# Values of three retention heads by a two-level product scheme, and a third of the convolution's taps on other engines

## The chip, the cores and the metric

The kernel runs on one core of a Trainium2 chip. Such a core has a matrix engine (TensorE, PE in the profile, its weight loads as PEld), three engines for element-wise work (VectorE as DVE, ScalarE as ACT, GpSimd as POOL), and queues that start DMA transfers (those of SyncE, SP, and those that GpSimd issues). Matrix products go to PSUM, where the kernel keeps eight tiles of 128 partitions x 512 float32; all other data are in SBUF. The metric is the device time of one execution, as the median of several runs.

## The reference

Two layers of a mixer block on x of 512 tokens x 1024 channels, in float32. In each layer h = RMSNorm(x), one input projection of h feeds three branches, and an output projection adds to x:

```
v = a * sigmoid(b);  y = depthwise conv of v, 31 taps, + bias;  layer norm, silu, * silu(gate)
retention, 4 heads:  q, k of 256 channels (rotary), v of 512 channels;
    o = sum over all tokens of (q.k) * decay(distance) * v;  normalised, * silu(gate)
attention, 16 heads of 64 in 4 groups, window of 128 tokens on both sides, with sinks
x = x + W_out( g0 * W_conv y_conv + g1 * W_ret y_ret + g2 * W_attn y_attn )
```

What the change touches are the values v of the retention heads, v[token, channel] = sum over the 1024 input channels of h[token, i] * W[i, channel], 512 channels a head; and the convolution, for each channel a sum of 31 products of a tap's weight with the shifted v.

## The kernel before

**Data.** Activations lie with channels on the partitions: eight tiles of 128 channels x 512 tokens for x, h and so on. To keep float32 accuracy with matmul operands of type float32r, every operand is split in a high part (`hh`, `wh`: a cast by ScalarE) and a low part (`hl`, `wl`: the rest), and `mm3()` makes three matmuls of each product: high x high, high x low, low x high.

**Weights.** `raw()` loads a weight tile of 128 x 1024 from HBM through SyncE's queue into pool `wraw` (four buffers). `split()` makes `wh` and `wl` of 512 columns each (eight buffers per pool): ScalarE casts, then VectorE subtracts. For kinds listed in `BY_DMA` the subtraction goes another way: ScalarE writes the negated high part into `wl`, and a DMA issued by GpSimd adds the raw weights to it.

**Products.** `columns()` gives 128 channels x 512 tokens: weights are the loaded (stationary) operand, 512 tokens move. `tokens()` gives 128 tokens x 512 channels for each of four token blocks: the activations are loaded, the weights move, 8 k-tiles x 4 blocks x 3 matmuls of 512 columns. `two()` makes two `columns()` results at once by a Strassen scheme in Winograd's form: seven products instead of eight, on halves of the tokens (256 moving columns) and halves of the input channels, with sums of weights made by VectorE in pool `ws` and sums of activations (`th_`, `tl_`) made once per layer in `sums()`. Three PSUM tiles a, b, e are used again within a call: b for the second, fifth and seventh product, after VectorE has read the one before.

**Retention.** `head()` runs four times a layer. Head 0 takes its values by `tokens()` from the unnormalised input and scales them later. Heads 1 to 3 (the second to fourth) call `queries()` (two `two()` calls and rotary), then `tokens()` and `split_values()`, then `toeplitz()` for the decay table (two tiles of pool `wide`), score products, value products, a normalisation (GpSimd makes the reciprocal root) and a gate. Between these steps stand filler pieces of other work, placed by `HEAD_FILL`: convolution input C, convolution taps T, gates R, S, L, K and so on.

**Convolution.** `taps()` runs for each of eight channel groups a layer: it fetches v into `pad` (one buffer, with zero borders set by GpSimd), and VectorE makes 31 multiply-adds one after the other into `yt`. `conv_stats()` later reads all eight results in the attention stage, and `conv_finish()` in the layer's last stage.

**The order.** The program records all operations first. The class `Plan` then runs a model of five engines with its own prices (`cost()`) and puts each engine's operations in a fixed order: always the ready one with the lowest priority number, which is the TensorE time planned so far plus an offset (`SPLIT_EARLY`, `EVAC_EARLY`, `LOAD_EARLY` make it earlier, `TAPS_LATE` of 150,000 ns makes the taps fill whatever is free). A tile gets a buffer of its pool in the order of the program. On the chip every engine works through its fixed list in order and waits where an operand is not there; all instructions carry the line of `issue()` (L342), so rows are told apart by tile names.

Of the kernel before, what the change touches and what calls it, by code (L numbers as in the profile page):

```python
# [13 lines left out]
AF = mybir.ActivationFunctionType  # L14
ALU = mybir.AluOpType
# [7 lines left out]
TAPS = 31  # L23
PADW = S + TAPS - 1
HALF_TAPS = TAPS // 2


POOLS = {"big": 12, "pp": 8, "mid": 2, "th": 2, "wide": 2, "pad": 1, "yt": 2, "wraw": 4, "wh": 8, "wl": 8, "ws": 2, "half": 3}
PSUM_POOLS = {"pc": 4, "ps": 4}
# [26 lines left out]

BY_DMA = ("xs", "or", "a22")

# [101 lines left out]
class Plan:  # L160
# [23 lines left out]
    def cost(self, engine, method, kw):  # L184
# [14 lines left out]
        if engine == "gpsimd":  # L199
            if kw.get("op") == ALU.pow:  # L200
                return 290 + 166 * n
            return 75 + 2.25 * n
        if method in ("bn_stats", "tensor_reduce"):
# [175 lines left out]
class Builder:  # L379
# [37 lines left out]

    def th(self):
        return self.tile("th", [P, S])

    def half(self):
# [14 lines left out]

    def raw(self, key):
        nc, i = self.nc, len(self.keys)
        self.keys.append(key)
        raw = self.tile("wraw", [P, 1024])  # L440
        with nc.urgency(2 * FIRST + FIRST_STEP * (i - 0.1) if i < 4 else LOAD_EARLY):
            nc.sync.dma_start(out=raw, in_=self.io["wpk"][i])
        return raw
# [22 lines left out]
    def two(self, col0, col1, out0, out1, func0=None, func1=None):  # L466
# [53 lines left out]
        if func1 is not None:  # L520
            nc.scalar.activation(out=out1, in_=out1, **func1)


# [130 lines left out]
    def take(self, k):  # L654

        nc = self.nc
        u = self.t2()
        nc.vector.tensor_scalar(out=u, in0=self.x[k], scalar1=self.ng[:, k:k + 1], scalar2=None, op0=ALU.mult)
        self.hilo(self.uh[k], self.ul[k], u)
        with nc.urgency(SQUARES_LATE):  # L660
            if k == 0:
                nc.scalar.activation(out=self.acc, in_=self.x[k], func=AF.Square)
            else:
                sq = self.th()
                nc.scalar.activation(out=sq, in_=self.x[k], func=AF.Square)
                nc.vector.tensor_tensor(out=self.acc, in0=self.acc, in1=sq, op=ALU.add)
# [91 lines left out]
    def conv_in(self, c):  # L758

        nc = self.nc  # L760
        th = self.th()
        v = self.pp()
# [4 lines left out]
    def taps(self, c):  # L767

        nc, prm = self.nc, self.prm
        pad = self.tile("pad", [P, PADW])  # L770
        y = self.tile("yt", [P, S])
        nc.gpsimd.memset(ap=pad[:, 0:HALF_TAPS], constant=0.0)
        nc.gpsimd.memset(ap=pad[:, HALF_TAPS + S:PADW], constant=0.0)
        self.fetch("vd", c, pad[:, HALF_TAPS:HALF_TAPS + S])
        with nc.urgency(TAPS_LATE):
            for k in range(TAPS):
                w = prm[:, O_DW + c * TAPS + k:O_DW + c * TAPS + k + 1]
                if k == 0:
                    nc.vector.tensor_scalar(out=y, in0=pad[:, k:k + S], scalar1=w, scalar2=prm[:, O_CB + c:O_CB + c + 1], op0=ALU.mult, op1=ALU.add)
                else:  # L780
                    nc.vector.scalar_tensor_tensor(out=y, in0=pad[:, k:k + S], scalar=w, in1=y, op0=ALU.mult, op1=ALU.add)
            self.keep("y", c, y)
# [21 lines left out]
    def head(self, h, first):  # L804
# [10 lines left out]
        else:  # L815
            qk = self.queries(h, self.cos, self.sin)
            v = self.split_values(self.tokens(R_V + h * 512))
        (qkh, qkl), (vh, vl) = qk, v
# [125 lines left out]
    def conv_finish(self):  # L944
# [3 lines left out]
        for k in range(8):  # L948
            th = self.th()
            y = self.fetch("yc", k, self.tile("yt", [P, S]))  # L950
# [86 lines left out]
    def attention(self):  # L1037
# [6 lines left out]
        def AG(c):  # L1044
            th = self.th()
            p = self.proj(A_GATE + c * P)
# [211 lines left out]
```

## Time and profile before

| | |
|---|---|
| median of 3 runs | 1946.38 us (1946.09 to 1947.39) |
| profiled execution, its own time | 1945.19 us |
| its span, first to last instruction | 1943.4 us |
| granted TensorE clock | 1.000 |
| busy: PE / PEld / DVE / ACT / POOL | 1927.2 / 1716.9 / 1692.2 / 1160.5 / 227.3 us |
| HBM read, written | 237.25 MB, 58.72 MB |

The times of instructions are from one profiled execution. A group row reads: line, engine, operation, output tile <- input tiles, shapes, count | busy us, mean ns of one | idle us of the engine just before them and what ended it. Wait rows give who waited for whom, us in total, how often, and the longest. Rows of the chain of waits give start, length and the work. A matmul's duration overlaps with its neighbour's, so that its cost in a stream is the spacing of starts. In the profile a float32r operand may be shown as f32.

### The profile page before, as it was taken

Reading aid. Unit: us, or ns where it says so; the run is one execution under the profiler, and the core shown is the slowest. Engines: PE = TensorE matmul, PEld = TensorE weight load, DVE = VectorE, ACT = ScalarE, POOL = GpSimd, SP = SyncE. Lnnn points to the kernel's source line nnn. Section 1 sums busy time; section 2 is a strip of 40 time slices with the busy share of each in tenths; the row PEclk is TensorE's granted clock in tenths of the full one; section 3 lists DMA queues with packets and bytes.
Section 4 is the critical chain, followed back from the end, with each engine's and each line's share of the span. In section 5 each row is a group of like instructions: output and inputs, shape, how many; then the busy total and the mean of one; then the engine's idle time right before and its main releaser. Section 6 shows DMA issues by size and latency. Waiting matters only on the chain.

```text
span 1943.4 us, 32881 instructions
## 1 busy us (share of the span) xinstructions
PE 1927.2 (99%) x11812; PEld 1716.9 (88%) x11812; DVE 1692.2 (87%) x3122; ACT 1160.5 (60%) x2230; POOL 227.3 (12%) x284
## 2 busy tenths in 40 slices
PE   8999999999999999999999999999999999999999
PEld 6899999999988888888889999999899888888887
DVE  8989998899998898987688999989999888989862
ACT  6565565556556577964436555655565465779531
POOL 0001011110123010100000010111101240100000
PEclk9999999999999999999999999999999999999999
DMA  6377478865769623488523665787656796134871
GB/s 234 91 210 192 130 217 213 216 163 177 201 168 234 217 76 98 155 271 286 168 91 109 211 178 149 209 217 211 166 177 178 197 232 203 66 112 160 281 250 70
DMA packets 143875, 348.98 MB, mean 180 GB/s; under 512 B 16096, under 2 KB 16352, under 8 KB 143712
## 3 DMA queue, kind: packets, MB, share of 16 engines
q1 hardware_dynamic: 115776, 296.02, 45.4%
q0 software_dynamic: 27936, 50.87, 15.2%
q8 instruction: 92, 1.51, 0.3%
q14 instruction: 71, 0.58, 0.1%
HBM read 237.25 MB, written 58.72 MB: 152 GB/s over the span
## 4 chain that ended last, share of the span: by engine, by line
PE 93%; DVE 3%; DMA 1%; ACT 1%; issue 1%; SPq 0%; POOLq 0%
PE pc L342 58%; PE ps L342 35%; DVE yt L342 1%; DMA wraw<-wpk 1%; DVE ws L342 1%; DVE wl L342 0%; DVE wide L342 0%; ACT wide L342 0%; DVE pp L342 0%; DVE big L342 0%; DMA wl<-wraw 0%; ACT pp L342 0%; DMA big<-xT 0%; ACT big L342 0%; DVE qk_v L342 0%
## 5 line engine op out<-in xcount | busy, mean ns | idle before, releaser
L342 PE MATMUL pc<-big,wh 128*128 128x256 f32 (+1 forms) x4848 | 1145.9, 327 | 0.4 <-DVE pp L342 0.3
L342 PEld LDWEIGHTS pc<-big,wh 128*128 128x128 f32 x4848 | 809.2, 188 | 79.9 <-issue 1.4
L342 PE MATMUL pc<-big,wl 128*128 128x256 f32 (+1 forms) x2424 | 789.1, 326 | 0.0
L342 ACT CAST wh<-wraw 128x512 fp32r<-128x512 f32 x558 | 343.6, 620 | 393.0 <-PE pc L342 215.3
L342 PEld LDWEIGHTS pc<-big,wl 128*128 128x128 f32 x2424 | 454.7, 188 | 36.4 <-issue 0.5
L342 DVE SCALAR_TENSOR_TENSOR yt<-pad,prm,yt 128x512 f32<-128x512 f32 x480 | 358.1, 746 | 4.2
L342 PE MATMUL ps<-wh,big 128*128 128x512 f32 (+1 forms) x1152 | 297.6, 347 | 7.2 <-ACT big L342 7.2
L342 DVE TENSOR_TENSOR wl<-wraw,wh 128x512 fp32r<-128x512 f32 x364 | 246.7, 685 | 25.2 <-ACT wh L342 22.9
L342 POOL DMA_DIRECT2D wl<-wraw x194 | 169.0, 880 | 841.9 <-ACT wl L342 507.6
L342 ACT CAST wh<-ws 128x512 fp32r<-128x512 f32 x264 | 162.2, 621 | 157.8 <-PE pc L342 83.4
L342 PEld LDWEIGHTS ps<-wh,big 128*128 128x128 f32 x1152 | 199.5, 189 | 36.9 <-ACT big L342 7.2
L342 PE MATMUL ps<-wl,big 128*128 128x512 f32 (+1 forms) x576 | 199.1, 346 | 0.0
L342 DVE TENSOR_TENSOR wl<-ws,wh 128x512 fp32r<-128x512 f32 x264 | 177.4, 685 | 5.6 <-ACT wh L342 4.8
L342 PE MATMUL ps<-big,wh 128*128 128x256 f32 x832 | 151.3, 279 | 0.0
L342 ACT ACTIVATE wl<-wraw 128x512 fp32r<-128x512 f32 x194 | 122.2, 630 | 13.7 <-PE ps L342 13.7
L342 PEld LDWEIGHTS ps<-big,wh 128*128 128x128 f32 x832 | 127.0, 188 | 0.2
L342 PEld LDWEIGHTS ps<-wl,big 128*128 128x128 f32 x576 | 108.7, 189 | 14.8 <-DVE wl L342 0.3
L342 PE MATMUL ps<-big,wl 128*128 128x256 f32 x416 | 116.0, 279 | 0.0
L342 DVE TENSOR_TENSOR ws<-wraw 128x512 f32<-128x512 f32 x132 | 86.8, 684 | 16.6 <-DMA wraw<-wpk 16.6
L342 PE MATMUL ps<-big 128*128 128x512 f32 (+2 forms) x448 | 100.4, 345 | 0.8 <-DVE sm_m L342 0.5
L342 PEld LDWEIGHTS ps<-big 128*128 128x128 f32 x448 | 81.7, 188 | 17.0 <-DVE big L342 1.1
L342 DVE TENSOR_TENSOR ws<-ws,wraw 128x512 f32<-128x512 f32 x132 | 90.2, 684 | 0.1
(124 smaller groups left out, 2084.7 us busy)
## 6 DMA issues: line engine op xcount, KB each, us to landing
wraw<-wpk SPq DMA_DIRECT2D x312, 512.0 KB, 3.9
wl<-wraw POOLq DMA_DIRECT2D x194, 256.0 KB, 5.6
g<-pp SPq DMA_DIRECT2D x48, 256.0 KB, 3.9
pp<-g SPq DMA_DIRECT2D x48, 256.0 KB, 4.7
rg<-pp SPq DMA_DIRECT2D x32, 256.0 KB, 3.0
pp<-rg SPq DMA_DIRECT2D x32, 256.0 KB, 4.6
yt<-y SPq DMA_DIRECT2D x32, 256.0 KB, 2.7
wide<-toe SPq DMA_DIRECT2D x16, 448.0 KB, 3.3
```

The lines of the kernel that those rows point to most:

```text
L342: getattr(getattr(self.nc, op.engine), op.method)(**kw)
```

## The change

Heads 1 to 3 call the new `tokens2()` instead of `tokens()`. It makes the same 512 tokens x 512 channels by the seven products of `two()`'s scheme, with the roles turned: the activation halves (128 tokens of `hh` or of the sums `th_`) are loaded, and the 256-column weight blocks move. Each product fills two PSUM tiles (two token blocks of its half), 2 x 4 k-tiles x 3 matmuls. The weights are four raw tiles (one of them in pool `wide`), four sums over 1024 columns by VectorE, and seven splits of two halves each; four of the seven (k1, k4, k5, k7) go by ScalarE and GpSimd's accumulating DMA, three (k2, k3, k6) by ScalarE and VectorE. The results are combined from PSUM into seven tiles of pool `pp`, from which `split_values()` then makes its parts.

In `taps()` VectorE keeps taps 0 to 20. For the last ten taps ScalarE multiplies the shifted input by the tap's weight, the first into `yz`, the others into `yp` (one buffer each), and GpSimd adds `yp` to `yz` nine times; VectorE adds `yz` to its sum at the end.

The pool `th` (two tiles of 128 x 512) is given up for `yz` and `yp`: the tanh and silu tiles come from `mid`, the squares of `take()` from `pp`. The planner's price of a GpSimd operation is changed.

```diff
@@ -23,9 +23,10 @@
 TAPS = 31
...
+POOL_TAPS = 10
...
-POOLS = {"big": 12, "pp": 8, "mid": 2, "th": 2, "wide": 2, "pad": 1, "yt": 2, "wraw": 4, "wh": 8, "wl": 8, "ws": 2, "half": 3}
+POOLS = {"big": 12, "pp": 8, "mid": 2, "wide": 2, "pad": 1, "yt": 2, "yz": 1, "yp": 1, "wraw": 4, "wh": 8, "wl": 8, "ws": 2, "half": 3}
...
-BY_DMA = ("xs", "or", "a22")
+BY_DMA = ("xs", "or", "a22", "v1", "v5", "v7")
...
-            return 75 + 2.25 * n
+            return 75 + 2.86 * n
...
-    def th(self):
-        return self.tile("th", [P, S])
...
-    def raw(self, key):
+    def raw(self, key, pool="wraw"):
...
-        raw = self.tile("wraw", [P, 1024])
+        raw = self.tile(pool, [P, 1024])
...
+    def tokens2(self, col):
+        nc = self.nc
+        a22 = self.raw(("q", self.l, col + 256, 1), "wide")
+        a21, a11, a12 = (self.raw(("q", self.l, col + c, i)) for c, i in ((256, 0), (0, 0), (0, 1)))
+        hs, ts = (self.hh, self.hl), (self.th_, self.tl_)
+        early = lambda: nc.urgency(EVAC_EARLY)
+        def add(a, b, out=None):
+            out = self.tile("ws", [P, 1024]) if out is None else out
+            with nc.urgency(SUM_EARLY):
+                nc.vector.tensor_tensor(out=out, in0=a, in1=b, op=ALU.add)
+            return out
+        def both(src, dma):
+            return [self.split(src[:, i:i + 512], dma) for i in (0, 512)]
+        def product(p, w, x, row, side, first=False):
+            for i in range(2):
+                tt = slice(side + i * P, side + (i + 1) * P)
+                for j in range(4):
+                    c = slice((j % 2) * 256, (j % 2 + 1) * 256)
+                    self.mm3(p[i][:, 0:256], tuple(v[row + j][:, tt] for v in x), (w[j // 2][0][:, c], w[j // 2][1][:, c]), first and j == 0, j == 3, not first)
+        k1 = both(a11, "v1" in BY_DMA)
+        s3 = add(a11, a21)
+        s1 = add(a21, a22, a21)
+        s2 = add(s1, a11)
+        k2 = both(s2, "v2" in BY_DMA)
+        k3 = both(s1, "v3" in BY_DMA)
+        k4 = both(a12, "v1" in BY_DMA)
+        k5 = both(s3, "v5" in BY_DMA)
+        s4 = add(s2, a12, s2)
+        k6 = both(s4, "v6" in BY_DMA)
+        k7 = both(a22, "v7" in BY_DMA)
+        a, b = [self.ps(), self.ps()], [self.ps(), self.ps()]
+        e = [self.pc(), self.pc()]
+        out = [self.pp() for t in range(4)]
+        t1, v2, t51 = [self.pp() for i in range(3)]
+        lo, hi = slice(0, 256), slice(256, 512)
+        half = (lo, hi)
+        product(a, k1, hs, 0, 0, True)
+        for i in range(2):
+            with early():
+                nc.scalar.copy(out=t1[:, half[i]], in_=a[i][:, lo])
+        product(b, k2, ts, 4, 256, True)
+        for i in range(2):
+            with early():
+                nc.vector.tensor_tensor(out=v2[:, half[i]], in0=b[i][:, lo], in1=t1[:, half[i]], op=ALU.add)
+        product(e, k3, ts, 0, 0, True)
+        for i in range(2):
+            with early():
+                nc.vector.tensor_tensor(out=t51[:, half[i]], in0=e[i][:, lo], in1=t1[:, half[i]], op=ALU.add)
+        product(a, k4, hs, 4, 0)
+        for i in range(2):
+            with early():
+                nc.scalar.copy(out=out[i][:, lo], in_=a[i][:, lo])
+        product(b, k5, ts, 0, 256)
+        for i in range(2):
+            with early():
+                nc.vector.scalar_tensor_tensor(out=out[2 + i][:, hi], in0=b[i][:, lo], scalar=-1.0, in1=t51[:, half[i]], op0=ALU.mult, op1=ALU.subtract)
+        product(e, k6, hs, 4, 256)
+        for i in range(2):
+            with early():
+                nc.vector.tensor_tensor(out=out[2 + i][:, lo], in0=e[i][:, lo], in1=v2[:, half[i]], op=ALU.add)
+        product(b, k7, ts, 4, 0)
+        for i in range(2):
+            with early():
+                nc.vector.scalar_tensor_tensor(out=out[i][:, hi], in0=b[i][:, lo], scalar=-1.0, in1=t1[:, half[i]], op0=ALU.mult, op1=ALU.subtract)
+        return out
...
         y = self.tile("yt", [P, S])
+        z = self.tile("yz", [P, S])
         nc.gpsimd.memset(ap=pad[:, 0:HALF_TAPS], constant=0.0)
         nc.gpsimd.memset(ap=pad[:, HALF_TAPS + S:PADW], constant=0.0)
         self.fetch("vd", c, pad[:, HALF_TAPS:HALF_TAPS + S])
         with nc.urgency(TAPS_LATE):
             for k in range(TAPS):
                 w = prm[:, O_DW + c * TAPS + k:O_DW + c * TAPS + k + 1]
+                own = k >= TAPS - POOL_TAPS
                 if k == 0:
                     nc.vector.tensor_scalar(out=y, in0=pad[:, k:k + S], scalar1=w, scalar2=prm[:, O_CB + c:O_CB + c + 1], op0=ALU.mult, op1=ALU.add)
+                elif not own:
+                    nc.vector.scalar_tensor_tensor(out=y, in0=pad[:, k:k + S], scalar=w, in1=y, op0=ALU.mult, op1=ALU.add)
+                elif k == TAPS - POOL_TAPS:
+                    nc.scalar.activation(out=z, in_=pad[:, k:k + S], func=AF.Copy, scale=w)
                 else:
-                    nc.vector.scalar_tensor_tensor(out=y, in0=pad[:, k:k + S], scalar=w, in1=y, op0=ALU.mult, op1=ALU.add)
+                    p = self.tile("yp", [P, S])
+                    nc.scalar.activation(out=p, in_=pad[:, k:k + S], func=AF.Copy, scale=w)
+                    nc.gpsimd.tensor_tensor(out=z, in0=z, in1=p, op=ALU.add)
+            nc.vector.tensor_tensor(out=y, in0=y, in1=z, op=ALU.add)
             self.keep("y", c, y)
...
-            v = self.split_values(self.tokens(R_V + h * 512))
+            v = self.split_values(self.tokens2(R_V + h * 512))
...
-                sq = self.th()
+                sq = self.pp()
...
-        th = self.th()
+        th = self.t2()
...
```

More of the change, by code (lines that the diff above doesn't have):

```diff
@@ L948, in conv_finish @@
         for k in range(8):
-            th = self.th()
+            th = self.t2()
             y = self.fetch("yc", k, self.tile("yt", [P, S]))
@@ L1044, in AG @@
         def AG(c):
-            th = self.th()
+            th = self.t2()
             p = self.proj(A_GATE + c * P)
```

## The prediction

> **What bounds the kernel now.** I read the totals of the page first, then its chain, then TensorE's waits.
>
> ```profile
> span 1943.4 us, 32881 instructions
> PE 1927.2 (99%) x11812; PEld 1716.9 (88%) x11812; DVE 1692.2 (87%) x3122; ACT 1160.5 (60%) x2230; POOL 227.3 (12%) x284
> ...
> PE 93%; DVE 3%; DMA 1%; ACT 1%; issue 1%; SPq 0%; POOLq 0%
> ```
>
> TensorE is busy for all but 16.2 us of the span, and 93% of the chain that ended last is its own. A busy matmul engine could still hide short gaps, so the waits are the second witness:
>
> ```profile
> PE ps L342 <- ACT big L342: 7.2, 1, 7.2
> PE ps L342 <- DVE pp L342: 3.0, 5, 0.9
> PE ps L342 <- DVE sm_m L342: 1.1, 3, 0.6
> ```
>
> The three largest come to 11.3 us, and 7.2 of them are one wait at the start. So the time is the sum of TensorE's spacings: a change gains what it takes off these, and loses what it makes TensorE wait. There is almost no old stall to win back, but VectorE at 87% is a near second bound. Stretch by stretch (PE, PEld, DVE, ACT, POOL busy us):
>
> ```profile
> 205.59:792.00 586.41, 584.15 (x3802) 529.80 (x3801) 533.06 (x993) 363.15 (x711) 93.29 (x113) 1.00 0.63 176
> 1170.00:1760.00 590.00, 588.36 (x3825) 533.52 (x3824) 534.28 (x998) 367.81 (x723) 92.42 (x114) 1.00 0.63 176
> 428.27:515.68 87.41, 87.41 (x678) 84.54 (x677) 82.00 (x150) 54.94 (x99) 12.26 (x16) 1.00 0.61 175
> ```
>
> The first two hold nearly all of what changes, one per layer. VectorE is busy 533 of 586 us there, and 82 of 87 in the third, which is mostly `two()` products. GpSimd is nearly free and ScalarE has a third left.
>
> **TensorE: the values of heads 2 to 4.** A `tokens()` call is 8 x 4 x 3 = 96 matmuls of 512 columns. A `tokens2()` call is 7 products x 2 x 4 x 3 = 168 matmuls of 256, the count and width of two `two()` calls. The chain shows a stretch of each:
>
> ```profile
> 173.77 21.93 PE ps L342 x94
> ...
> 221.96 19.79 PE pc L342 x168
> ...
> 405.87 22.40 PE ps L342 x96
> ```
>
> The old call takes 22.40 us (233 ns a matmul; the 94 records of 21.93 give the same rate). At the 117.8 ns of the x168 stretch, the new one takes 19.79 us. That saves 2.61 us a head, and over six heads (three per layer) 15.7 us. But in `two()` the weights are loaded and the tokens move; in `tokens2()` it is the other way round. That order exists in the q projection of attention, 256 wide:
>
> ```profile
> 598.72 0.39 PE L342 MATMUL ps<-wh,big 128*128 128x256 f32 x2
> ...
> 600.75 0.39 PE L342 MATMUL ps<-wh,big 128*128 128x256 f32 x2
> ```
>
> 18 matmuls start in 2.03 us there, 113 ns each; 168 of them take 18.95 us and the gain becomes 20.7 us. Both ends stand for the range. I take 16, near the lower end, because that row is from the heads' own stage. I see no loss from the larger number of weight loads: the x168 stretch has as many.
>
> **VectorE, ScalarE, GpSimd: the taps.** The costs come from these groups (count, busy us, mean ns):
>
> ```profile
> L342 DVE SCALAR_TENSOR_TENSOR yt<-pad,prm,yt 128x512 f32<-128x512 f32 x480 | 358.1, 746 | 4.2
> L342 DVE TENSOR_TENSOR wl<-ws,wh 128x512 fp32r<-128x512 f32 x264 | 177.4, 685 | 5.6 <-ACT wh L342 4.8
> L342 DVE SCALAR_TENSOR_TENSOR pp<-pc,half 128x256 f32<-128x256 f32 x132 | 55.6, 421 | 12.1 <-PE pc L342 9.6
> L342 DVE TENSOR_TENSOR ws<-ws,prm 128x1024 f32<-128x1024 f32 x10 | 12.2, 1218 | 0.0
> L342 ACT CAST wh<-ws 128x512 fp32r<-128x512 f32 x264 | 162.2, 621 | 157.8 <-PE pc L342 83.4 <-PE ps L342 30.0 <-DVE ws L342 28.8
> L342 ACT COPY half<-pc 128x256 f32<-128x256 f32 x66 | 24.3, 368 | 4.0 <-PE pc L342 3.7
> L342 ACT ACTIVATE th<-yt,prm 128x512 f32<-128x512 f32 x16 | 11.2, 722 | 6.9 <-DVE yt L342 6.8
> L342 POOL DMA_DIRECT2D wl<-wraw x194 | 169.0, 880 | 841.9 <-ACT wl L342 507.6 <-DVE yt L342 87.6 <-DVE big L342 41.9
> L342 POOL TENSOR_TENSOR qk_r<-qk_v,mhalf 128x16 f32<-128x16 f32 x10 | 29.9, 2994 | 104.2 <-DVE qk_v L342 104.2
> ```
>
> Sixteen channel groups give up ten VectorE taps each, 160 x 0.746 = 119.4 us, and take one sum back, 16 x 0.685 = 11.0. ScalarE gains 160 scaled copies with a per-partition operand; the row with such an operand is 722 ns, so 115.5 us. GpSimd gains 144 adds of 128x512, which no row shows. The floor is VectorE's same add, 0.685 us (99 us in all); the ceiling is GpSimd's slowest two-input row, 2.99 us (431 us). I take 1.54 us (222 us), between them, which is also the price the diff sets in the planner (75 + 2.86 x 512), a setting and not a measurement. GpSimd comes to 227 + 222 = 449 us, 23% of the span; even the ceiling gives 34%.
>
> **The same engines: `tokens2()`.** VectorE adds four sums over 1024 columns (4 x 1.218), six subtractions for k2, k3, k6 (6 x 0.685) and ten evacuations of 256 columns (10 x 0.421): 13.2 us a head, 79.1 in all. Net for VectorE: 11.0 + 79.1 - 119.4 = -29.3 us. ScalarE gets six more casts and four copies: 6 x 0.621 + 4 x 0.368 = 5.2 us a head, 31 in all; with the taps 1160 + 147 = 1307 us, 68%. GpSimd's accumulating transfers stay eight a head (k1, k4, k5, k7, two halves each), and SyncE's weight loads stay four. All this lies beside TensorE, so it costs nothing while VectorE stays under it: about 533 - 15 = 518 of 578 us per layer. If that cover goes, rival C is its price.
>
> **What may become late.** `wh` and `wl` have eight buffers and a product now takes two of each, so a split can start only when the product four places earlier has ended, three products (8.5 us) before its own matmuls. `tokens()` had three weights of 24 matmuls ahead, 16.8 us. The transfer path in the trace:
>
> ```profile
> 395.94 0.63 ACT L342 CAST wh<-wraw 128x512 fp32r<-128x512 f32 x1 [0.26 <-ACT wl L342]
> ...
> 397.39 0.86 POOL L342 DMA_DIRECT2D wl<-wraw  x1 [0.55 <-ACT wl L342]
> ...
> 399.03 0.86 POOL L342 DMA_DIRECT2D wl<-wraw  x1 [0.78 <-DVE yt L342]
> ...
> DMA to landing us min/median/max: 3.2/5.6/9.6
> ```
>
> From cast to landing is 1.45 + 5.6 = 7.1 us; the second half is issued 1.6 us later, 8.7 us against the 9.2 it has (it is first read six matmuls on). So the slack is 1.4 and 0.5 us. One GpSimd add of 1.54 us ahead of the issue uses it up, and a landing of 9.6 us comes 3 to 4 us late. k4, k5 and k7 are such products, 18 in all. Against that, the planner may put k6, which goes by VectorE, before k5. From 0 to 18 x 2 = 36 us; I take 3, as most issues should find no add in front. What waits behind a late add on GpSimd's queue is these transfers, the reciprocal roots and the sink copies of attention; the roots are followed by filler products, so 1.5 us there costs nothing. ScalarE can be held too, since `yp` is one buffer: a tap copy waits for the add before it, and the casts and evacuations behind it wait as well. They have 2.8 us (24 x 117.8 ns) until their bank is reused; free up to there, beyond it part of the 36.
>
> **The scratch pool.** Tanh tiles move to `mid` (two buffers), squares to `pp` (eight, of which `tokens2()` takes seven). Only the `two()` call before a score stage meets another user of `mid`: one or two waits of about one 0.7 us op per layer. Between 0 and some 5 us; I take 2.
>
> **Sum.** The profiled execution took 1945.19 us, 1.8 beside its span, and lies 1.2 under the median. 1945.2 - 16 + 3 + 2 = 1934.2 on its own scale, and **1935** as a median.
>
> **Rivals.** A is the forecast. B: the late splits take most of the gain, 18 x 0.8 = 14 us, so 1944; for it speaks the 0.5 us of slack, against it that TensorE hardly waits today in `two()`, whose last matrix uses the same path with 9.9 us ahead (seven products of twelve matmuls). C ends slower: GpSimd's adds hold up VectorE. Each stretch has room for 578 - 518 = 60 us over 72 adds, so it decides from 0.83 us of delay per add; at 1.0 us VectorE is 12 us over per layer and the time is 1930 + 24, about 1955; at the whole 1.54 us it is 51 over, about 2033. The nearest row is a long GpSimd instruction under which two-input VectorE taps ran:
>
> ```profile
> 731.68 2.90 POOL L342 TENSOR_TENSOR qk_r<-qk_v,mhalf 128x16 f32<-128x16 f32 x1 [14.45 <-DVE qk_v L342]
> ...
> 732.05 0.75 DVE L342 SCALAR_TENSOR_TENSOR yt<-pad,prm,yt 128x512 f32<-128x512 f32 x1
> ...
> 733.25 0.75 DVE L342 SCALAR_TENSOR_TENSOR yt<-pad,prm,yt 128x512 f32<-128x512 f32 x1
> ```
>
> Both taps kept their 0.75 us while GpSimd was in its own instruction, so no hold for its whole length is seen; but it reads only 16 elements, where an add reads 2 x 512. So C gets 0.17. [...]
>
> D: the change doesn't do what it says, the matmuls not getting cheaper, because weight loads bind in this order of operands or because the tap chain (nine add steps in a row) ends late and holds the convolution's statistics. With no gain and the same stalls it is 1951.
>
> **How the numbers follow.** A 0.62, B 0.13, C 0.17, D 0.08. A alone spans 1927 (20.7 us gained, little lost) to 1939. The range takes in B, D and the start of C: 1927 to 1954; C beyond 1954 and the corners are left out. About 0.2%, 3.9 us, is what a measurement can tell from no change, so between 1942.5 and 1950.3 is the same. A counts as faster; B mostly as same, a third as faster; C as slower; D as slower or same. Faster 0.66, same 0.11, slower 0.23.
>
> **What would show it.** In the changed profile: stretches of 168 matmuls of 256 columns in 19 to 20 us in the heads; VectorE near 1663 us and ScalarE near 1307; no new line among TensorE's waits over some 5 us. Against A: matmuls waiting on `wl` (B), VectorE's two-input taps or subtractions longer than 0.75 and 0.69 us while GpSimd adds (C). A GpSimd add far over 1.5 us makes C and the late splits likelier.

## The result, and the profile after

The changed kernel takes **2009.63 us** (median of 4 runs, 2008.94 to 2010.69); the kernel before took 1946.24 us beside it (1945.11 to 1947.39). The ratio is 1.0325, with a 95% interval from 1.031 to 1.034: slower by 63 us. The forecast was 1935 us, in a range from 1927 to 1954 us. The prediction was wrong in sign and far outside its range.

The totals of the changed kernel, and the shares of the chain that ended last:

```profile
span 2008.9 us, 34030 instructions
...
PE 1933.3 (96%) x12244; PEld 1732.8 (86%) x12244; DVE 1774.2 (88%) x3098; ACT 1279.7 (64%) x2448; POOL 446.4 (22%) x428
...
PE 52%; DVE 20%; issue 4%; DMA 4%; SPq 0%; ACT 0%; POOL 0%; DVEq 0%; POOLq 0%
```

TensorE is idle for 75.6 us of the span; before, it was 16.2. VectorE was expected near 1663 us and is at 1774, although it has fewer instructions than before. Its share of the chain went from 3% to 20%. ScalarE (1280, expected 1307) and GpSimd (446, expected 449) are close to their sums. TensorE's waits say who it stands for (us in total, times, longest):

```profile
PE pc L343 <- DVE pp L343: 28.9, 24, 2.7
PE pc L343 <- DVE half L343: 8.8, 10, 2.2
PE ps L343 <- ACT big L343: 6.9, 1, 6.9
PE ps L343 <- DVE sm_m L343: 6.5, 5, 1.6
...
PE pc L343 <- DMA wl<-wraw: 1.6, 1, 1.6
```

The first two lines are evacuations of PSUM by VectorE that come late; before, the first of them was

```profile
PE pc L342 <- DVE pp L342: 0.3, 1, 0.3
```

and the second wasn't there. The transfers of late splits, rival B, are 1.6 us. The next view is the page's costliest groups (count, busy us, mean ns):

```profile
L343 DVE TENSOR_TENSOR wl<-wraw,wh 128x512 fp32r<-128x512 f32 x376 | 272.0, 733 | 20.5 <-ACT wh L343 19.0
L343 DVE SCALAR_TENSOR_TENSOR yt<-pad,prm,yt 128x512 f32<-128x512 f32 x320 | 285.4, 892 | 3.8
L343 POOL TENSOR_TENSOR yz<-yz,yp 128x512 f32<-128x512 f32 x144 | 223.3, 1551 | 252.2 <-ACT yp L343 246.0
...
L343 DVE TENSOR_TENSOR wl<-ws,wh 128x512 fp32r<-128x512 f32 x288 | 209.1, 746 | 2.5 <-ACT wh L343 1.9
```

A tap grew from 746 to 892 ns on average, a split of `ws` from 685 to 746. These rows have two SBUF tiles as inputs. Taps alone account for 320 x 0.146 = 46.7 us. Over all VectorE groups, count times growth of the mean comes to 123.5 us, or **0.86 us for each of the 144 GpSimd adds**. 1663 + 123.5 = 1786, 12 more than the 1774 measured: neighbouring records overlap, so that durations add up to more than busy time. By busy time it is 1774 - 1663 = 111 us, 0.77 for each. So the price of an add is about 0.8 us. The timeline of one head shows how it happens (start, us):

```profile
392.95 1.39 POOL L343 TENSOR_TENSOR yz<-yz,yp 128x512 f32<-128x512 f32 x1 [0.91 <-ACT yp L343]
393.11 1.78 DVE L343 SCALAR_TENSOR_TENSOR yt<-pad,prm,yt 128x512 f32<-128x512 f32 x1
...
395.39 1.28 POOL L343 TENSOR_TENSOR yz<-yz,yp 128x512 f32<-128x512 f32 x1 [1.05 <-ACT yp L343]
395.42 0.41 DVE L343 SCALAR_TENSOR_TENSOR pp<-pc,half 128x256 f32<-128x256 f32 x1
395.75 1.47 DVE L343 SCALAR_TENSOR_TENSOR yt<-pad,prm,yt 128x512 f32<-128x512 f32 x1
```

The first tap starts 0.16 us into an add and ends at 394.89, 0.55 us after the add's end at 394.34. The second ends at 397.22, again 0.55 us after its add's end at 396.67. The timeline lists 31 taps singly that start inside an add; all 31 end 0.54 to 0.56 us after it. So a tap that meets an add gets on only when the add is over. The evacuation at 395.42 reads PSUM and only one SBUF tile; it kept its 0.41 us inside an add. One form with a single SBUF input was held all the same. A TENSOR_SCALAR of 128x4 on `sm_m`, 0.16 us otherwise, took 1.25 us and ended at 695.08, 0.03 us after the add:

```profile
693.29 1.76 POOL L343 TENSOR_TENSOR yz<-yz,yp 128x512 f32<-128x512 f32 x1 [5.19 <-ACT yp L343]
693.83 1.25 DVE L343 TENSOR_SCALAR sm_m<-sm_m 128x4 f32<-128x4 f32 x1
```

The stage where this costs most is the heads. First the kernel before, then the changed one (PE, PEld, DVE, ACT, POOL busy us; then granted clock):

```profile
300.00:400.00 100.00, 99.70 (x714) 93.48 (x713) 89.60 (x155) 59.88 (x111) 16.70 (x23) 1.00 0.79 208
```

```profile
300.00:400.00 100.00, 90.35 (x632) 82.78 (x631) 95.20 (x139) 64.27 (x119) 42.20 (x39) 1.00 0.74 197
```

VectorE is busier by 5.6 us with 16 fewer instructions, and TensorE has lost 9.35 us.

### The profile page after: what moved, and what is told of

It reads as the page before. It is cut to its first block, busy times and chain, and to the rows that moved or that the text cites. A ratio compares the mean times of both kernels' runs of the same rounds, so it can differ in the third digit from the quotient of the medians.

```text
span 2008.9 us, 34030 instructions
## 1 busy us (share of the span) xinstructions
PE 1933.3 (96%) x12244; PEld 1732.8 (86%) x12244; DVE 1774.2 (88%) x3098; ACT 1279.7 (64%) x2448; POOL 446.4 (22%) x428
## 3 DMA queue, kind: packets, MB, share of 16 engines
q0 software_dynamic: 27936, 50.87, 14.7%
## 4 chain that ended last, share of the span: by engine, by line
PE 52%; DVE 20%; issue 4%; DMA 4%; SPq 0%; ACT 0%; POOL 0%; DVEq 0%; POOLq 0%
PE pc L343 34%; PE ps L343 18%; DVE yt L343 6%; DVE wl L343 3%; DVE ws L343 3%; DVE pp L343 2%; DVE big L343 2%; DVE wide L343 2%; DMA wl<-ws 1%; DMA md<-pp 1%; DVE mid L343 1%; DVE half L343 1%; DMA yc<-yt 1%; DMA wraw<-wpk 0%; DMA pad<-vd 0%
## 5 line engine op out<-in xcount | busy, mean ns | idle before, releaser
L343 ACT CAST wh<-ws 128x512 fp32r<-128x512 f32 x300 | 183.3, 622 | 175.1 <-PE pc L343 99.5
L343 DVE TENSOR_TENSOR wl<-wraw,wh 128x512 fp32r<-128x512 f32 x376 | 272.0, 733 | 20.5 <-ACT wh L343 19.0
L343 DVE SCALAR_TENSOR_TENSOR yt<-pad,prm,yt 128x512 f32<-128x512 f32 x320 | 285.4, 892 | 3.8
L343 POOL TENSOR_TENSOR yz<-yz,yp 128x512 f32<-128x512 f32 x144 | 223.3, 1551 | 252.2 <-ACT yp L343 246.0
L343 PE MATMUL ps<-wh,big 128*128 128x256 f32 (+1 forms) x1248 | 262.7, 306 | 9.3 <-ACT big L343 6.9
L343 DVE TENSOR_TENSOR wl<-ws,wh 128x512 fp32r<-128x512 f32 x288 | 209.1, 746 | 2.5 <-ACT wh L343 1.9
L343 PE MATMUL ps<-wl,big 128*128 128x256 f32 (+1 forms) x624 | 190.1, 306 | 0.3 <-DMA wl<-wide 0.3
L343 DVE TENSOR_TENSOR ws<-wraw 128x512 f32<-128x512 f32 (+1 forms) x144 | 110.2, 787 | 15.8 <-issue 8.1
L343 ACT ACTIVATE yp<-pad,prm 128x512 f32<-128x512 f32 x144 | 104.0, 722 | 19.9 <-POOL yz L343 19.5
L343 DVE TENSOR_TENSOR ws<-ws,wraw 128x512 f32<-128x512 f32 (+1 forms) x138 | 109.5, 793 | 0.0
```

The lines of the kernel that those rows point to most:

```text
L343: getattr(getattr(self.nc, op.engine), op.method)(**kw)
```

## The experiments

**Theories.** Theory 1: GpSimd's adds hold VectorE because they read SBUF (rival C's mechanism). Theory 2: the +79 us of the values don't fit beside TensorE, whatever GpSimd does. Rival B and the scratch pool are the other suspects. The kernel before takes 1946 us in each comparison.

### The scratch pool alone

```diff
-POOLS = {"big": 12, "pp": 8, "mid": 2, "th": 2, "wide": 2, "pad": 1, "yt": 2, "wraw": 4, "wh": 8, "wl": 8, "ws": 2, "half": 3}
+POOLS = {"big": 12, "pp": 8, "mid": 2, "wide": 2, "pad": 1, "yt": 2, "wraw": 4, "wh": 8, "wl": 8, "ws": 2, "half": 3}
...
-                sq = self.th()
+                sq = self.pp()
...
-        th = self.th()
+        th = self.t2()
...
```

> The kernel before with only the scratch pool th given up: tanh and silu tiles from mid, squares from pp; values and taps as before. All theories: 1946 within 0.3% (I had charged 2 us, at most 5). If it is over 1955, part of the other kernels' loss belongs to the pool.

The last replacement stands in three places. 1950.47 us, ratio 1.0021 [1.0012, 1.0031]. The pool costs 3.7 us; I charged 2, with 5 as the upper end.

### One half of the change at a time

In the first kernel all 31 taps go by VectorE again and the three heads keep `tokens2()`; in the second the ten taps stay moved and the heads use `tokens()`. Both are without the pool `th`, like the change, so its 3.7 us are in both.

```diff
-                elif not own:
+                else:
                     nc.vector.scalar_tensor_tensor(out=y, in0=pad[:, k:k + S], scalar=w, in1=y, op0=ALU.mult, op1=ALU.add)
-                elif k == TAPS - POOL_TAPS:
-                    nc.scalar.activation(out=z, in_=pad[:, k:k + S], func=AF.Copy, scale=w)
-                else:
-                    p = self.tile("yp", [P, S])
-                    nc.scalar.activation(out=p, in_=pad[:, k:k + S], func=AF.Copy, scale=w)
-                    nc.gpsimd.tensor_tensor(out=z, in0=z, in1=p, op=ALU.add)
-            nc.vector.tensor_tensor(out=y, in0=y, in1=z, op=ALU.add)
...
```

> The new values alone: tokens2() as in the changed kernel, all 31 taps back on VectorE, no GpSimd adds. Theory 1 (GpSimd's adds block VectorE's two-input instructions, and everything else of the change is harmless): VectorE keeps its old durations (taps 0.746 us, subtractions 0.685 us), its busy time is 1692 + 79 = 1771 us by instruction counts, which fits under TensorE's 1930; time 1930 to 1940. Theory 2 (VectorE has too little room for the sums of tokens2(), whoever else works): time 1950 to 1985, with TensorE waiting for VectorE in the heads. Theory 3 (the halved lead of the transferred splits): TensorE waits on wl by DMA, 10 us or more in sum.

```diff
-            v = self.split_values(self.tokens2(R_V + h * 512))
+            v = self.split_values(self.tokens(R_V + h * 512))
```

> The tap offload alone: ten taps by ScalarE and GpSimd as in the changed kernel, but the values of all heads by tokens(). VectorE's own work falls by 108 us against the kernel before. Theory 1 (each GpSimd add costs VectorE about 0.86 us, 124 us in all): VectorE ends at about 1692 - 108 + 124 = 1708 us, so the offload gives nothing to VectorE, but late instructions make TensorE wait in places: time 1950 to 1980. Theory 2 (the sums of tokens2() are the trouble): time within 0.5% of before.

Values only: 2002.73 us, 1.0298 [1.0274, 1.0322]. Taps only: 2022.45 us, 1.0385 [1.0367, 1.0402]. Each half loses by itself, 57 and 76 us, both more than the ranges above had it, and together they lose 63, so the parts don't add up. The values-only kernel has no longer VectorE instruction (taps 745 ns), so theory 2 holds for a part as well. The chain of that kernel also shows the new products' rate:

```profile
175.29 5.45 PE ps L343 x48
```

Those are the first two products of a call, with k1 and k2, 113.5 ns a matmul: a call takes 168 x 113.5 = 19.07 us, 3.33 less than the old 22.40. Over six heads this is 20.0 us, the upper end of the predicted 15.7 to 20.7. So TensorE's gain is real, and rival D is not what happened.

### Is it the reading, and how much per instruction?

The kernel before, with `th` given up and 144 GpSimd instructions put between the taps that work on two scratch tiles; what they write enters no result. Three forms: an add (two SBUF inputs), a copy (one), a memset (none).

```diff
+                if k >= TAPS - 9:
+                    nc.gpsimd.tensor_tensor(out=self.z, in0=self.z, in1=self.p, op=ALU.add)
```

> The kernel before with nothing moved, and 144 GpSimd adds of 128x512 on two scratch tiles of their own, nine beside the last nine taps of each channel group; nothing reads their result (the pool th is given up as in the change, to make room). Theory 1: the adds alone lengthen VectorE's two-input instructions by 0.7 to 0.9 us per add, 100 to 130 us; VectorE would be at 1800 to 1820 us and the time 1985 to 2050. Without blocking: 1946 within 0.3%, VectorE 1692.

```diff
-                    nc.gpsimd.tensor_tensor(out=self.z, in0=self.z, in1=self.p, op=ALU.add)
+                    nc.gpsimd.tensor_copy(out=self.z, in_=self.p)
```

> As the run with 144 scratch adds beside the unchanged work, but each GpSimd instruction is a copy of one 128x512 tile to another (one SBUF input). Nothing reads the result. If GpSimd's reading blocks VectorE's two-input instructions, the copies block too, in proportion to their length: VectorE's busy time rises by 144 x 0.4 to 0.8 us, 60 to 115 us, and the time by as much, 2005 to 2060. If only GpSimd's second input does it: 1946 within 0.3%.

```diff
-                    nc.gpsimd.tensor_tensor(out=self.z, in0=self.z, in1=self.p, op=ALU.add)
+                    nc.gpsimd.memset(ap=self.z, constant=0.0)
```

> The same with 144 GpSimd memsets of 128x512, which write but read nothing; nothing reads the result. If it is the reading that blocks: time 1946 within 0.3%, VectorE 1692 us. If any GpSimd access or its writing blocks: VectorE's busy time up by 144 x 0.5 = 70 us or more and the time above 1990.

Adds: 2073.19 us, 1.0649 [1.0633, 1.0665]. Copies: 1977.01 us, 1.0157 [1.0140, 1.0174]. Memsets: 1962.81 us, 1.0084 [1.0069, 1.0099]. Group rows of the three, in this order:

```profile
L342 POOL TENSOR_TENSOR yz<-yz,yp 128x512 f32<-128x512 f32 x144 | 232.7, 1616 | 9.7
...
L342 DVE TENSOR_TENSOR wl<-wraw,wh 128x512 fp32r<-128x512 f32 x364 | 270.4, 751 | 26.1 <-ACT wh L342 24.3 <-PE ps L342 0.8
```

```profile
L342 DVE TENSOR_TENSOR wl<-wraw,wh 128x512 fp32r<-128x512 f32 x364 | 252.5, 702 | 26.6 <-ACT wh L342 24.5 <-PE ps L342 0.8
...
L342 POOL COPY yz<-yp 128x512 f32<-128x512 f32 x144 | 142.4, 989 | 7.6
```

```profile
L342 DVE TENSOR_TENSOR wl<-wraw,wh 128x512 fp32r<-128x512 f32 x364 | 246.7, 686 | 25.9 <-ACT wh L342 24.0 <-PE ps L342 0.8
...
L342 POOL MEMSET yz<- 128x512 f32 x145 | 77.7, 536 | 8.5 <-POOLq L1250 0.3
```

VectorE's busy time rises over the pool-only kernel (1692.4) by 132.2 us with adds, 37.3 with copies and 3.8 with memsets: 0.92, 0.26 and 0.03 us for each GpSimd instruction. The totals without and with the adds:

```profile
PE 1930.0 (99%) x11812; PEld 1715.7 (88%) x11812; DVE 1692.4 (87%) x3122; ACT 1161.2 (60%) x2230; POOL 230.6 (12%) x284
```

```profile
PE 1971.6 (95%) x11812; PEld 1742.1 (84%) x11812; DVE 1824.6 (88%) x3122; ACT 1160.0 (56%) x2230; POOL 457.2 (22%) x430
```

It's the reading that holds VectorE; a GpSimd write of the same tile takes next to nothing from it. An add with its two inputs is also twice as long as a copy (shortest 1.26 against 0.61 us), so these runs don't tell the number of inputs from the length. With adds the time rises by 122.7 us (2073.19 - 1950.47), nearly the 132, though not by VectorE alone: the first root on GpSimd (`tr_r`) starts at 37.9 us in place of 23.0, and the mean granted clock is 0.982. These adds, on which nothing waits, all ran in the first 361 us and so came denser than in the change. The adds ended 23 us above the range of the first theory, the copies between their two forecasts. The memset kernel missed its expectation of no difference by 12 us over the pool-only kernel. In its first 50 us TensorE is busy 34.25 us, against 43.12 in the pool-only kernel, with two waits of 8.8 us in all on `pp` by VectorE. The memsets stand on GpSimd's queue ahead of the first root, which starts at 35.7 us in place of 23.0, so that loss is queueing, not blocking.

### The change without the long reads

The same kernel in the same order (the planner is still charged the old price), but each GpSimd add takes only the first column; the sums of the other 511 tokens are left out.

```diff
-            return 75 + 2.86 * n
+            return 75 + 2.86 * (S if n == 1 else n)
...
-                    nc.gpsimd.tensor_tensor(out=z, in0=z, in1=p, op=ALU.add)
+                    nc.gpsimd.tensor_tensor(out=z[:, 0:1], in0=z[:, 0:1], in1=p[:, 0:1], op=ALU.add)
```

> The changed kernel in its own order (the planner is given the old price for them), but each of the 144 GpSimd adds works on the first column of yz and yp alone; the sums of the other 511 tokens are left out. Every wait, transfer and VectorE instruction of the change stays; what goes is the reading of 128x512 tiles by GpSimd and the add's length. Theory 1 (the blocking of VectorE is the whole loss): VectorE's taps return to 0.746 us and its busy time to about 1660, TensorE's waits fall to some 15 us and the time to 1925 to 1940, below the kernel before. Theory 4 (the blocking is only part: splits with half the lead, the crowded pools, GpSimd's queue): 1950 to 1990.

1941.39 us, 0.9978 [0.9966, 0.9989].

```profile
PE 1912.0 (99%) x12244; PEld 1724.7 (89%) x12244; DVE 1660.5 (86%) x3098; ACT 1274.7 (66%) x2448; POOL 287.5 (15%) x428
```

VectorE is at 1660.5 us, where the prediction's count of instructions had put it (1663). VectorE's busy time falls by 113.7 us against the changed kernel, 0.79 for each add, with every other instruction the same. So the long adds cost 2009.6 - 1941.4 = **68 us**, more than the whole loss; without them the change gains 4.6 us. This edit takes away the reading and the add's time on GpSimd's queue together. What speaks for the reading is VectorE's shorter busy time, and that the waits that fell are TensorE's waits for VectorE; TensorE's idle time went from 75.6 to 27.9 us. The result lies 1 us above the range of theory 1 and 6 us short of the forecast: the idle time is 11.7 us above that of before, where the prediction charged 5. TensorE's waits for VectorE on `pp` (8.3 us), `sm_m` (3.4) and `big` (3.1) come to 14.8 us, 4.1 before, and 11.3 of them lie in attention.

### The sums by accumulating transfers

```diff
-                    nc.gpsimd.tensor_tensor(out=z, in0=z, in1=p, op=ALU.add)
+                    nc.gpsimd.dma_start(out=z, in_=p, accum_op=ALU.add)
```

> The changed kernel, but each of the 144 adds of yp to yz is an accumulating DMA issued by GpSimd instead of an instruction of GpSimd; the same sums are computed. Theory 1 (GpSimd's reads block VectorE): VectorE's taps go back to 0.75 us and its subtractions to 0.69, its busy time to about 1663 us, and the time falls to 1930 to 1950. The ten taps of a channel group then take nine transfers of some 6 to 7 us in a row, 60 us, about the pace of the taps before, and GpSimd's queue gets 144 more issues of 0.88 us. If not the blocking but the tap chain's length or GpSimd's queue were the trouble: 2000 us or more.

2075.03 us, 1.0663 [1.0647, 1.0679]: it avoids the block (taps back at 746 ns, VectorE at 1672.1) and is slower still.

```profile
PE pc L343 <- DVE ws L343: 30.2, 2, 17.2
PE ps L343 <- DVE big L343: 20.4, 13, 3.0
```

A transfer lands 4.7 us after its issue (median), nine stand in a row for each group, and `yp` is one buffer. So the last `y` comes late, and the convolution's statistics with it: two waits of 30.2 us in all, one of 17.2. This is the late tap chain that rival D spoke of, in another kernel. It is a part of the loss only, for TensorE is idle for 106.3 us here. The order changed too: between a layer's first and last softmax rows (`sm_m`) VectorE has 66 and 67 pieces of work on `yt`, against 45 in both layers of the kernel with narrow adds. The shares of the two aren't shown.

### The planner told that VectorE is slower

The planner's prices are blind to the block. With VectorE's margin at 1.17 in place of 1.06 it sets its order as if VectorE were 10% slower; once on the taps-only kernel, once on the whole change.

```diff
-MARGIN = {"vector": 1.06, "scalar": 1.06}
+MARGIN = {"vector": 1.17, "scalar": 1.06}
```

> The tap offload alone (values by tokens()), with one more edit: the planner prices every VectorE operation 10% higher (margin 1.17 in place of 1.06), about what the blocking added. Theory 1a (the loss of 76 us lies in the fixed order: the plan, which knows nothing of the blocking, packs taps into every VectorE gap of the heads, so that each blocked stretch delays what TensorE needs, while VectorE idles later): with a fitting price the taps spread out, TensorE's waits on VectorE in the heads fall and the time comes to 1946 to 1985, VectorE still near 1712 us busy. Theory 1b (a blocked evacuation or subtraction stalls TensorE whatever the order): 2010 or more.

> The changed kernel with the planner's VectorE prices 10% higher (margin 1.17 in place of 1.06). Theory 1a (the order packs VectorE too tightly for the blocking): the waits of the heads shrink, but the change as a whole has more VectorE work than before (1692 - 29 + 124 = 1787 us), so the taps run into attention: 1985 to 2025, no clear gain over 2010, with TensorE's waits moved from the heads to attention. If the order alone were to blame: 1950 to 1980.

Taps only: 1993.02 us, 1.0237 [1.0222, 1.0253], so 29 of the 76 us come back, between the two forecasts. The whole change: 2050.99 us, 1.0536 [1.0520, 1.0552], 41 us worse than without it and above both forecasts. What the margin did to its order can be counted, as each engine's order is fixed: between a layer's first and last softmax rows VectorE now has 73 and 77 pieces of work on `yt`, where the changed kernel has 45 and 45. So the taps that left the heads went into attention; how the 41 us follow from that was not traced. What the first did is seen in VectorE's work on `yt` from 100 to 560 us and from 700 to 800, first with the old margin, then with the new (us, count, clock):

```profile
100.00:560.00 460.00, 124.65 (x145) 0.99 0.64 178
...
700.00:800.00 100.00, 0.00 (x0) 1.00 0.24 80
```

```profile
100.00:560.00 460.00, 87.15 (x103) 1.00 0.67 184
...
700.00:800.00 100.00, 13.01 (x17) 1.00 0.28 91
```

With the old margin the taps were packed into the heads, where the adds held them; the new one spread them out, and TensorE's waits for `pp` fell from 36.9 to 11.7 us. So a fixed order made without the block is a part of the loss, not all of it.

### Why the values lose by themselves: VectorE's load, or their own products

Three more kernels with `tokens2()` in none, one or three heads of a layer. In two of them five taps a group, not ten, leave VectorE, summed by accumulating transfers; these two have seven `pp` buffers and one `th`, while the one-head kernel has no `th`, like the change. The line for one head; the others list heads 1 to 3, or none:

```diff
-            v = self.split_values(self.tokens2(R_V + h * 512))
+            v = self.split_values((self.tokens2 if h in (3,) else self.tokens)(R_V + h * 512))
```

> One head a layer by tokens2(), all 31 taps on VectorE. VectorE 1692 + 2 x 13.2 = 1718 us, TensorE 5.2 us less. Load theory: a part of the 57 us that three heads lost, about in proportion or less, 1950 to 1965 us. Rival (the 26 us more lie in VectorE's room, and only a full VectorE costs): 1939 to 1945 us.

> Three heads a layer by tokens2(), five taps by accumulating transfers. VectorE 1643 + 79 = 1722 us, as much as one head with all taps on VectorE, but TensorE 15.7 us less. Load theory: about the time of that kernel less 10 us, 1940 to 1960 us. Rival (the values cost by their own matmuls and splits, whatever VectorE's load): some 57 us above the kernel with five taps and no head, 1985 to 2000 us.

> No head by tokens2(), five taps of each group as ScalarE copies summed by accumulating transfers. VectorE by instructions: 1692 - 80 x 0.746 + 16 x 0.685 = 1643 us. Load theory (the time follows VectorE's load, since its order leaves little of its room usable): the 16.4 us that the version with one head gained are mostly those freed taps, so 1933 to 1937 us here, the 5 us of cheaper matmuls missing. Rival (the one head's matmuls made the gain): 1944 to 1948 us.

One head with all taps on VectorE: 1980.88 us, 1.0177 [1.0163, 1.0191]. Three heads with five taps moved: 1977.31 us, 1.0157 [1.0143, 1.0171]. No head with five taps moved: 1944.43 us, 0.9986 [0.9977, 0.9995]. The totals of one head and of three heads:

```profile
PE 1935.6 (98%) x11956; PEld 1722.8 (87%) x11956; DVE 1714.2 (87%) x3162; ACT 1166.2 (59%) x2246; POOL 230.5 (12%) x284
```

```profile
PE 1932.9 (98%) x12244; PEld 1735.1 (88%) x12244; DVE 1715.5 (87%) x3178; ACT 1230.9 (62%) x2368; POOL 286.6 (15%) x348
```

The two kernels load VectorE alike and take the same time within 4 us, though one has three times as many of the new products. And with three heads throughout, the time goes with VectorE's busy time: 2002.73 us at 1757.5 (all taps on VectorE), 1977.31 at 1715.5, 1941.39 at 1660.5 (the narrow adds), though the kernels differ in how taps leave VectorE. So most of the loss is the load. The rival by which the products cost by themselves (1985 to 2000 us for three heads) doesn't hold as it stands, but a smaller cost of that kind isn't excluded: four heads more (two a layer) should save 13.3 us of matmuls, and 3.6 show, though the scratch pools differ. Nor were the load theory's sizes right: these two lie 16 and 17 us above its ranges. The kernel with no head lies 7 us above, in its rival's range: VectorE time freed below the 1692 us of before gains almost nothing there. Added above it, it costs about itself or more: 26 us by instructions (22 in busy time) cost 34, of which the scratch pool may be 3.7, and used up the 6.7 that two heads' matmuls save. VectorE's work on `yt` in the attention stage shows the place: the kernel before, then one head, then all three with all taps on VectorE (us, count, granted clock):

```profile
700.00:800.00 100.00, 21.74 (x30) 1.00 0.29 95
```

```profile
700.00:800.00 100.00, 37.67 (x51) 0.91 0.26 85
```

```profile
700.00:800.00 100.00, 52.12 (x71) 0.85 0.21 69
```

Three heads with five taps moved:

```profile
700.00:800.00 100.00, 37.48 (x51) 0.86 0.33 93
```

The same 51 as one head with all taps. The added sums and splits push taps out of the heads, and they come out in attention, which has no room. The engines in the same stretch, before and with three heads:

```profile
700.00:800.00 100.00, 96.95 (x582) 83.93 (x581) 91.35 (x209) 79.50 (x185) 7.82 (x10) 1.00 0.29 95
```

```profile
700.00:800.00 100.00, 82.55 (x437) 67.75 (x437) 97.98 (x204) 55.26 (x126) 7.01 (x12) 0.85 0.21 69
```

VectorE is full there, TensorE waits for it (23.9 us in all on `big`, the largest line of this kernel's waits), and the granted clock falls as well, to 0.85.

### A version that beats both

`tokens2()` for the fourth head only, and five taps by accumulating transfers: the no-head kernel of above with one head more.

```diff
+POOL_TAPS = 5
...
+                    nc.gpsimd.dma_start(out=z, in_=p, accum_op=ALU.add)
...
+            v = self.split_values((self.tokens2 if h in (3,) else self.tokens)(R_V + h * 512))
```

> A version built on the finding: tokens2() for the fourth head of each layer alone, and five of 31 taps by ScalarE, summed by accumulating transfers instead of GpSimd's adds, so that nothing blocks VectorE; one th tile is kept, pp has seven. VectorE: 16 x (5 x 0.746 - 0.685) = 48.7 us less, 2 x 13.2 = 26.4 us more. TensorE: 2 x 2.6 = 5.2 us less. If VectorE's backlog at the end of attention is what sets the loss, the time is 1930 to 1943; if the transfers' chain or the pools get in the way, 1945 to 1960.

**1929.68 us** (1928.69 to 1931.6), 0.9913 [0.9899, 0.9926]: 16 us faster than before.

```profile
PE 1915.6 (99%) x11956; PEld 1717.3 (89%) x11956; DVE 1675.0 (87%) x3098; ACT 1209.1 (63%) x2326; POOL 285.1 (15%) x348
```

VectorE is at 1675 us, 17 below the kernel before, and only 21 pieces of work on `yt` fall between 700 and 800 us, where the kernel before has 30. Against the kernel with no head it gains 14.7 us. The cheaper matmuls give 2 x 3.33 = 6.7 of them, and in the profiled executions, which lie 11.0 us apart, TensorE's busy time is 7.4 us lower and its idle time 3.6. The remaining 3.7 us are within the spread of the two kernels' runs (1941.81 to 1945.62 and 1928.69 to 1931.6).

## Why the prediction was wrong, point by point

- **What bounds the kernel now.** Right as a reading. "VectorE at 87% is a near second bound" stood there, and the argument then didn't use it.
- **TensorE's saving**, 16 taken of 15.7 to 20.7: right in kind, the upper end is what the chain row shows (20.0).
- **Instruction counts.** Right: the 1663 us for VectorE were met within 3 us where the adds are short (1660.5). ScalarE and GpSimd came within 3% of their sums, and the add's 1.54 us, a setting, was measured as 1.55. That is luck: the shortest adds take 1.26 us, so the mean isn't the add's own length.
- **"All this lies beside TensorE, so it costs nothing while VectorE stays under it: about 533 - 15 = 518 of 578 us per layer."** This is the step that failed, in two ways. First, the 518 itself: every GpSimd add puts about 0.8 us on VectorE (0.79 in busy time against the narrow adds, 0.86 by durations), 114 to 124 us in all, which is more than the 108 us (119.4 - 11.0) that moving the taps frees. The prediction's sum had this term at nothing and left it to rival C. The narrow adds put the cost of the long adds at 68 us. Second, the room of 60 us a layer: it isn't cover. One head a layer adds 13 us of VectorE time to a layer's 533 and costs 17 us a layer (15 without the scratch pool), even with cheaper matmuls. An average over a stage hides that attention is at 91 of 100 and that the low-priority taps fall into it.
- **Rival C**, 0.17: its mechanism was the right one, but two of its parts were wrong. The nearest row was chosen by the length of the GpSimd instruction (2.90 us), and it reads only 16 elements; what holds VectorE is reading (0.92 us for each add, 0.03 for each memset), and no row before had a long read. And "decides from 0.83 us of delay per add" rests on the 60 us of room again. By that formula the 0.79 to 0.86 us measured would have cost 0 to 4 us; the adds cost 68. The far end of C, 2033, was nearer than the forecast, for a wrong reason: with 1.54 us an add and 60 us of cover. In these traces the taps end 0.55 us after the add that they met, the evacuation with one SBUF input isn't held (0.41 us inside an add), and memsets hold next to nothing; but the short TENSOR_SCALAR, also with one SBUF input, was held (1.25 us in place of 0.16). The measured price is under the add's full length: a tap starts some time into the add and ends 0.55 us after it, 0.2 less than its own length, so that the two taps shown lost 1.03 and 0.72 us; and about nine of the first layer's 72 adds met no instruction with two SBUF inputs.
- **Rival B**, 0.13, and the 3 us for late splits: TensorE's waits on transferred splits come to 1.6 us for `wl<-wraw`. Fallen.
- **Rival D**, 0.08: fallen for the matmuls; the late tap chain appears only where transfers do the sums.
- **Scratch pool**, 2 us of 0 to 5: 3.7 measured.
- **Chances.** With no row against rival C for a long read, and VectorE at 82 of 87 us in `two()`, the 0.17 was too low. The sign hung on a cost that no row bounded; the range left out the whole part of C that became true.

What stays open: why the parts don't add (57 and 76 alone, 63 together), beyond that fewer taps reach attention where ten were moved (27 pieces of work on `yt` from 700 to 800 us in the changed kernel, against 71 with values only); how much of the three heads' loss is the products' own; and how the 41 us of the wider margin follow from the taps that it puts into attention.

## What to carry to other kernels

Before moving work from VectorE to GpSimd, count what GpSimd's instructions read: here a 128x512 add took 0.8 to 0.9 us from VectorE, more than the 0.75 us of the tap that it replaced, while a write-only instruction took 0.03. Don't take a second engine's average room as cover: look in every stage, the fullest above all, for where low-priority work goes when it is displaced. And if no row speaks against a rival at the size in question, price it at its full effect, from the first microsecond.

## What the runs showed of the hardware that was not expected

- **GpSimd's reads.** For 128x512 fp32 among the same VectorE work, mean and shortest: add 1616 and 1255 ns, copy 989 and 609, memset 536 and 523. VectorE loses 0.92, 0.26 and 0.03 us to each.
- **After some stalls the granted clock was halved, to 0.50, and it stayed there while TensorE worked again.** The mean of 0.91 over 100 us in the one-head kernel is made of stretches of 4 us like these (TensorE busy us, count, granted clock, DMA share, GB/s):

```profile
740.00:744.00 4.00, 2.16 (x9) 1.00 0.00 0
744.00:748.00 4.00, 2.87 (x9) 0.67 0.00 0
748.00:752.00 4.00, 1.69 (x6) 0.50 0.00 0
752.00:756.00 4.00, 3.78 (x16) 0.55 0.00 0
756.00:760.00 4.00, 3.40 (x16) 1.00 0.19 42
```

TensorE is busy 3.78 us of the fourth stretch, at a granted clock of 0.55. So a stall can cost more than its length. In this kernel the idle time inside the span rises by 26.1 us (42.3 against 16.2), and the busy time by 8.4, though its matmuls should take 6.7 us less: some 15 us more, put down to slow matmuls. In the changed kernel from 300 to 400 us, stalls of about 2 us in every 16 to 20 us (TensorE busy for 2.08 of 4 us at the least) left the clock at 1.00; where TensorE was busy for 1.8 of 4 us, from 408 to 412 us, it was at 0.50 next. Every stretch below 1.00 in that kernel is at 0.50; these are the rows of the first, with the 4 us before it, and of the second:

```profile
408.00:412.00 4.00, 1.78 (x16) 1.00 0.04 14
412.17:415.58 3.41, 3.41 (x17) 0.50 0.00 0
835.42:842.25 6.83, 5.42 (x18) 0.50 0.64 217
```

In the one-head kernel the slow stretches can be bounded as well:

```profile
745.36:755.60 10.24, 7.47 (x25) 0.50 0.00 0
...
765.84:772.67 6.83, 4.59 (x15) 0.50 0.10 38
```

All four lengths are one, two or three times 3.41 us, within 0.01 us. What makes the clock change isn't shown.
